# Fewer and later loads at the start of a fused encoder layer: constants packed into two arrays, one token block loaded after the first weights, 14 warming products instead of 17

## The chip, the cores and the metric

The kernel runs on one core of a Trainium2 chip. The metric is the device time of one execution in microseconds (us), lower is better. Before the change three runs gave a median of 1285.72 us (1284.95 to 1287.09).

## The reference

One encoder layer on x of 1024 tokens by 1024 features, all in float32:

```python
h = rmsnorm(x, norm1_w)
z = h @ w_in                     # 2852 columns, split into
qa, c_kv, iq, ik, iw, qb, kb, vb, gb = split(z)
c = rmsnorm(c_kv, kv_norm_w)
ka = rmsnorm(c @ w_uk, k_norm_w); va = c @ w_uv
out_a = indexed_sparse_attention(rmsnorm(qa, q_norm_w), ka, va, iq, ik, iw, rel_bias)
y = chunkwise_retention(rotary(qb), rotary(kb), vb)
out_b = silu(gb) * (group_norm(y) * ret_gn_w + ret_gn_b)
x = x + concat(out_a, out_b) @ w_out
h2 = rmsnorm(x, norm2_w)
return x + (silu(h2 @ w_gate) * (h2 @ w_up)) @ w_down
```

The sparse attention scores keys with a small indexer (`iq`, `ik`, `iw`), keeps 256 of them per query and attends over these.

## The kernel before, in words

The tokens are eight blocks of 128 (`NB`), worked in two halves of four. A product in float32 is split into three: an operand is written as a rounded part and a rest (`Thi` and `Tlo` for tokens, `whi` and `wlo` for weights), and TensorE (PE) takes `whi,Thi`, `wlo,Thi` and `whi,Tlo`. ScalarE (ACT) makes the rounded parts, VectorE (DVE) the rests. For one block and one chunk of weight columns this is 8 steps over the features of three products each, 24 in all (`token_major`, L467).

The input projection (`in_proj`, L1018) goes chunk by chunk over the columns of `w_in`: first the chunk `idx` of 292 columns (the latent for keys and values, and the indexer), then chunks of 256 columns. In each chunk the four blocks follow one another. The weights of a chunk come in pieces over SyncE's DMA queue (SP) into three buffers `wraw` (`pieces`, L278); the first chunk has four pieces of 292 KB, of which the last goes into a buffer named `sc`. A later chunk has two pieces of 512 KB.

Each token block has two loads: its transposed halves `xt` of 256 KB each (`x_load`, L410), which ACT scales by the norm's weights `n1` into `Thi` and DVE into `Tlo` (`scale_in`, L398), and its plain rows, two of 256 KB into the tiles `maA` (`x_stats`, L442), of which ACT takes the sums of squares and GpSimd (POOL) the reciprocal roots `rstd`. The projection's results for `idx` are scaled by `rstd` into a tile `ci` (`post_idx`, L477), and `keys` (L489) makes the keys of a block from it: a transpose by the identity `eye`, scaling by `kvw` into `ct`, a product with `wukv`, the tile `kv`, its sums of squares on ACT, a root on DVE and POOL (`rc`), the tile `kn` on DVE and two more transposes on PE.

Before the first weights arrive, `first_loads` (L172) gives PE 17 products of a tile of zeros (`WARM`, L30; the tile is `junk`). `second_loads` (L188) issues the other early loads on SP and `constants2` (L217) the tables for later stages on ACT's queue. `roots` (L211) multiplies `kw` and `kvw` by constants on DVE.

The order within an engine is set in two steps. The kernel's own planner estimates clocks and interleaves threads of work (`tick`, `step`) with the main products. The framework under it then orders the instructions of each engine. Loads take turns at eight semaphores: each issue waits until the load eight places before it has landed, whichever of the two queues that was on. Every engine and each queue works strictly in its order.

Of the kernel before, what the change touches and what calls it, by code (L numbers as in the profile page):

```python
# [16 lines left out]
NB = 8  # L17
KT = 8
# [8 lines left out]
NEG = -1.0e30  # L27
BIG = 3.0e38
SUB = 2
WARM = 17  # L30
VALUES, PAIRS, GATES = 4, 4, 2


# [10 lines left out]
def host_constants():  # L44
    f = np.float32
    pos = np.arange(S, dtype=np.float64)
    inv = 10000.0 ** (-np.arange(32, dtype=np.float64) / 32)
    ang = (pos.astype(f)[:, None] * inv.astype(f)[None, :]).astype(np.float64)
    cos = np.cos(ang).astype(f).reshape(NB, 128, 32).transpose(1, 0, 2)
    sin = np.sin(ang).astype(f).reshape(NB, 128, 32).transpose(1, 0, 2)  # L50
    lg = np.log1p(-(2.0 ** (-5.0 - np.arange(H, dtype=np.float64))))
    dq = np.exp((pos + 1.0)[:, None] * lg[None, :])
    dk = np.exp(-(pos + 1.0)[:, None] * lg[None, :]) * DH ** -0.5
    dec = np.concatenate([dq, dk], axis=1).astype(f).reshape(NB, 128, 16).transpose(1, 0, 2)
    bits = np.tile((np.uint32(1) << np.arange(32, dtype=np.uint32))[None, :], (128, 1))
    eye = np.eye(128, dtype=f)
    return {
        "cos": np.ascontiguousarray(cos), "sin": np.ascontiguousarray(sin),
        "dec": np.ascontiguousarray(dec), "bits": bits, "eye": eye,
        "causal": np.triu(np.ones((128, 128), f)),  # L60
    }

# [11 lines left out]
def layouts(host):  # L74


    x = host["x"].reshape(NB, 128, KT, 128)
    near = np.ascontiguousarray(host["rel_bias"][buckets()].transpose(0, 2, 1))
    return {"xt": np.ascontiguousarray(x.transpose(0, 3, 2, 1)).reshape(NB, 128, KT * 128),
            "n1": np.ascontiguousarray(host["norm1_w"].reshape(KT, 128).T),  # L80
            "n2": np.ascontiguousarray(host["norm2_w"].reshape(KT, 128).T), "near": near}

# [37 lines left out]
class Layer:  # L120
# [51 lines left out]
    def first_loads(self):  # L172
# [10 lines left out]
        p = self.pd()  # L183
        for _ in range(WARM):
            nc.tensor.matmul(p, warm[:, :128], warm[:, :512], start=True, stop=True)
        self.x_load(1, (nc.scalar, nc.scalar))

    def second_loads(self):  # L188
        nc, a = self.nc, self.a
        self.stats(0)  # L190
        self.x_load(2, (nc.sync, nc.sync))
        self.sqk = self.st([128, NB, 16], tag="sqk")
        nc.sync.dma_start(self.sqk, a["dec"])
# [1 line left out]
        self.x_load(3, (nc.sync, nc.sync))  # L195
        for b in (2, 3):
            self.go("root", self.x_stats(b))
        self.eye = self.sb([128, 128], tag="eye")
        nc.sync.dma_start(self.eye, a["eye"])
        self.kvw = self.sb([128, 1], tag="kvw")  # L200
        nc.sync.dma_start(self.kvw, a["kv_norm_w"].rearrange("o p -> p o"))
        self.wukv = self.sb([128, 128], tag="wukv")
        nc.sync.dma_start(self.wukv[:, :64], a["w_uk"][0])
        nc.sync.dma_start(self.wukv[:, 64:], a["w_uv"][0])
        self.kw = self.sb([128, 1], tag="kw")
        self.qw = self.sb([128, 1], tag="qw")
        for s in range(2):
            nc.sync.dma_start(self.kw[64 * s:64 * s + 64], a["k_norm_w"].rearrange("o p -> p o"))
            nc.sync.dma_start(self.qw[64 * s:64 * s + 64], a["q_norm_w"].rearrange("o p -> p o"))

    def roots(self):  # L211

# [3 lines left out]

    def constants2(self):  # L217
        nc, a = self.nc, self.a
        self.cos = self.st([128, NB, 32], tag="cos")
        self.sin = self.st([128, NB, 32], tag="sin")  # L220
        nc.scalar.dma_start(self.cos, a["cos"])
        nc.scalar.dma_start(self.sin, a["sin"])
        self.causal = self.st([128, 128], tag="causal")
        nc.scalar.dma_start(self.causal, a["causal"])
        self.gnw = self.st([128, 512], tag="gnw")
# [1223 lines left out]
```

## Time and profile before

| | |
|---|---|
| median of 3 runs | 1285.72 us |
| lowest, highest | 1284.95, 1287.09 us |
| the profiled execution | 1285.11 us |
| its span, first to last instruction | 1283.2 us |
| TensorE busy | 1252.7 us (98%) |
| VectorE, ScalarE busy | 992.2 us (77%), 785.9 us (61%) |
| mean granted TensorE clock | 0.999 |
| DMA, mean over the span | 95 GB/s, 121.34 MB |

The profile is of one execution. Its page gives busy times per engine; the trace behind it can be asked for instructions in order of time, with the idle time just before each and what ended it, and for the busy time of every engine in a chosen stretch. TensorE's busy time is modelled from pipelined products, so a product's printed length overlaps the next one; the distance from start to start is the better measure. The kernel's line for nearly all instructions is that of a helper (L100 before, L102 in the changed kernel), so groups are told apart by tile names.

### The profile page before, as it was taken

What the parts mean: (1) busy time and instruction counts of PE and PEld (TensorE: products, weight loads), DVE (VectorE), ACT (ScalarE), POOL (GpSimd) and SP (SyncE); (2) the same over time, 40 slices, a digit from 0 to 9 for tenths busy, and PEclk for the clock granted to TensorE, in tenths of its full rate; (3) what the DMA queues carried; (4) which work ended last, traced back from release to release, by engine and by line L of the source; (5) the groups of instructions that cost most, each with busy time, mean ns of one, the idle gap of its engine ahead of it and who ended that gap; (6) DMA issues with size and microseconds to landing.
All of it is one profiled execution on the core that took longest, in us unless ns stands there. A gap on an engine that the chain in (4) does not pass through costs nothing.

```text
span 1283.2 us, 22661 instructions
## 1 busy us (share of the span) xinstructions
PE 1252.7 (98%) x8369; PEld 1125.7 (88%) x8369; DVE 992.2 (77%) x2584; ACT 785.9 (61%) x1764; POOL 57.9 (5%) x68
## 2 busy tenths in 40 slices
PE   8999999999999999999999999999989999999998
PEld 6899998999999887888888878888988989898997
DVE  5889999888978887778887686545489787777883
ACT  7778986555795795588568834423385354444551
POOL 0501011010020000000000000000000000000000
PEclk9999999999999999999999999999999999999999
DMA  8523214221242223222222222225434242323302
GB/s 294 157 73 101 67 46 116 67 67 34 67 148 67 67 83 94 70 66 84 82 68 72 91 66 81 84 68 200 144 98 149 67 132 78 120 84 115 99 33 83
DMA packets 156895, 121.34 MB, mean 95 GB/s; under 512 B 7280, under 2 KB 136944, under 8 KB 156656
## 3 DMA queue, kind: packets, MB, share of 16 engines
q1 hardware_dynamic: 151744, 111.14, 28.9%
q10 hardware_dynamic: 5040, 8.74, 1.9%
q8 instruction: 66, 1.08, 0.4%
q14 instruction: 45, 0.37, 0.1%
HBM read 115.67 MB, written 4.19 MB: 93 GB/s over the span
## 4 chain that ended last, share of the span: by engine, by line
PE 59%; DVE 18%; ACT 14%; issue 5%; DMA 3%; POOL 1%; ACTq 0%; POOLq 0%; SPq 0%; DVEq 0%
PE d L100 50%; PE t L100 7%; ACT junk L100 6%; DVE wlo L100 4%; ACT whi L100 2%; PE l L100 2%; DVE L L100 2%; DMA wraw<-in_w_in_dram 1%; DVE S L100 1%; DVE Tlo L100 1%; ACT waste L100 1%; ACT Thi L100 1%; DVE th L100 1%; DVE wraw L100 1%; DVE junk L100 1%
## 5 line engine op out<-in xcount | busy, mean ns | idle before, releaser
L100 PE MATMUL d<-whi,Thi 128*128 128x256 f32 (+2 forms) x1136 | 349.5, 308 | 3.6 <-ACT whi L100 1.4
L100 PE MATMUL d<-wlo,Thi 128*128 128x256 f32 (+2 forms) x1136 | 340.0, 299 | 1.6 <-DVE wlo L100 1.6
L100 PE MATMUL d<-whi,Tlo 128*128 128x256 f32 (+2 forms) x1136 | 339.8, 299 | 0.0
L100 PEld LDWEIGHTS d<-whi,Thi 128*128 128x128 f32 x1136 | 214.2, 189 | 17.2 <-ACT Thi L100 2.2
L100 ACT ACTIVATE whi<-wraw 128x512 fp32r<-128x512 f32 (+1 forms) x300 | 172.8, 618 | 84.6 <-PE d L100 62.3
L100 PEld LDWEIGHTS d<-wlo,Thi 128*128 128x128 f32 x1136 | 214.5, 189 | 10.1 <-DVE wlo L100 2.3
L100 PEld LDWEIGHTS d<-whi,Tlo 128*128 128x128 f32 x1136 | 214.5, 189 | 8.7 <-DVE Tlo L100 1.2
L100 DVE TENSOR_TENSOR wlo<-wraw,whi 128x512 fp32r<-128x512 f32 (+1 forms) x302 | 197.2, 674 | 12.6 <-ACT whi L100 12.2
L100 ACT ACTIVATE junk<-sc,tc 128x384 bf16<-128x384 f32 (+5 forms) x186 | 163.5, 879 | 35.6 <-DVE tc L100 32.9
L100 PE MATMUL d<-Phi,wlo 128*128 128x256 f32 x616 | 170.8, 278 | 3.0 <-DVE wlo L100 3.0
L100 PE MATMUL d<-Phi,whi 128*128 128x256 f32 x616 | 171.3, 279 | 1.3 <-ACT u L100 1.0
L100 PE MATMUL d<-Plo,whi 128*128 128x256 f32 x616 | 170.7, 278 | 0.0
L100 PE MATMUL d<-Thi,whi 128*128 128x512 f32 (+1 forms) x368 | 143.0, 389 | 0.0
L100 PE MATMUL d<-Tlo,whi 128*128 128x512 f32 (+1 forms) x368 | 141.4, 385 | 1.3 <-DVE Tlo L100 1.3
L100 PE MATMUL d<-Thi,wlo 128*128 128x512 f32 (+1 forms) x368 | 141.4, 384 | 0.0
L100 PEld LDWEIGHTS d<-Phi,wlo 128*128 128x128 f32 x616 | 115.5, 188 | 3.7 <-DVE wlo L100 3.6
L100 PEld LDWEIGHTS d<-Phi,whi 128*128 128x128 f32 x616 | 115.9, 188 | 2.5 <-ACT u L100 1.7
L100 PEld LDWEIGHTS d<-Plo,whi 128*128 128x128 f32 x616 | 115.6, 188 | 0.3
L100 DVE TENSOR_TENSOR x<-d,x 128x512 f32<-128x512 f32 (+1 forms) x56 | 33.9, 614 | 64.5 <-PE d L100 56.7
L100 ACT ACTIVATE whi<-S 128x1024 fp32r<-128x1024 f32 x44 | 45.6, 1057 | 60.4 <-PE d L100 47.4
L100 PEld LDWEIGHTS d<-Thi,wlo 128*128 128x128 f32 x368 | 69.1, 188 | 14.8
L100 PEld LDWEIGHTS d<-Tlo,whi 128*128 128x128 f32 x368 | 69.2, 188 | 13.7 <-DVE Tlo L100 1.6
(331 smaller groups left out, 2349.0 us busy)
## 6 DMA issues: line engine op xcount, KB each, us to landing
wraw<-in_w_down_dram SPq DMA_DIRECT2D x44, 512.0 KB, 3.7
wraw<-in_w_in_dram SPq DMA_DIRECT2D x24, 512.0 KB, 3.7
wraw<-in_w_gate_dram SPq DMA_DIRECT2D x44, 256.0 KB, 3.1
wraw<-in_w_up_dram SPq DMA_DIRECT2D x44, 256.0 KB, 3.5
quad<-in_w_gate_dram SPq DMA_DIRECT2D x44, 256.0 KB, 3.6
quad<-in_w_up_dram SPq DMA_DIRECT2D x44, 256.0 KB, 4.0
wraw<-in_w_in_dram SPq DMA_DIRECT2D x32, 256.0 KB, 3.4
wraw<-in_w_out_dram SPq DMA_DIRECT2D x16, 512.0 KB, 4.2
```

The costliest lines, as they stand in the source:

```text
L100: return f(*args, **kw)
```

## The change

Eight loads of small constants (`eye`, `kvw`, the halves of `wukv`, and `kw` and `qw` twice each) become one array `few` of 128 by 259, put together on the host and loaded once. `cos` and `sin` become one array `turn`, and its load goes from ACT's queue to SP's. The two loads of token block 1 go from ACT's queue, before the weights' consumers, to SP's queue behind the four pieces of the first chunk. `WARM` goes from 17 to 14.

```diff
-WARM = 17
+WARM = 14
...
+    twice = lambda w: np.concatenate([w, w], axis=1).T
+    few = np.concatenate([np.eye(128, dtype=np.float32), host["w_uk"][0], host["w_uv"][0], host["kv_norm_w"].T,
+                          twice(host["k_norm_w"]), twice(host["q_norm_w"])], axis=1)
...
         for _ in range(WARM):
             nc.tensor.matmul(p, warm[:, :128], warm[:, :512], start=True, stop=True)
-        self.x_load(1, (nc.scalar, nc.scalar))
 
     def second_loads(self):
         nc, a = self.nc, self.a
+        self.x_load(1, (nc.sync, nc.sync))
         self.stats(0)
+        few = self.sb([128, 259], tag="few")
+        nc.sync.dma_start(few, a["few"])
+        self.eye, self.wukv = few[:, :128], few[:, 128:256]
+        self.kvw, self.kw, self.qw = [few[:, i:i + 1] for i in (256, 257, 258)]
         self.x_load(2, (nc.sync, nc.sync))
...
-        self.eye = self.sb([128, 128], tag="eye")
-        nc.sync.dma_start(self.eye, a["eye"])
-        self.kvw = self.sb([128, 1], tag="kvw")
-        nc.sync.dma_start(self.kvw, a["kv_norm_w"].rearrange("o p -> p o"))
-        self.wukv = self.sb([128, 128], tag="wukv")
-        nc.sync.dma_start(self.wukv[:, :64], a["w_uk"][0])
-        nc.sync.dma_start(self.wukv[:, 64:], a["w_uv"][0])
-        self.kw = self.sb([128, 1], tag="kw")
-        self.qw = self.sb([128, 1], tag="qw")
-        for s in range(2):
-            nc.sync.dma_start(self.kw[64 * s:64 * s + 64], a["k_norm_w"].rearrange("o p -> p o"))
-            nc.sync.dma_start(self.qw[64 * s:64 * s + 64], a["q_norm_w"].rearrange("o p -> p o"))
...
-        self.cos = self.st([128, NB, 32], tag="cos")
-        self.sin = self.st([128, NB, 32], tag="sin")
-        nc.scalar.dma_start(self.cos, a["cos"])
-        nc.scalar.dma_start(self.sin, a["sin"])
+        turn = self.st([128, 2, NB, 32], tag="turn")
+        nc.sync.dma_start(turn, a["turn"])
+        self.cos, self.sin = turn[:, 0], turn[:, 1]
```

The order of instructions moves on every engine up to the first chunks of the projection; TensorE's differs in some 430 rows at its head (of 7735 before and 7726 now) and is the same after them. Three places matter below.

First, SP's queue ahead of the second chunk of weights. Before, from the loads of token block 3 (`mb__171`, `mb__172`) to `qw`; the same two small loads `kw` and `qw` come once more and then the first piece of the second chunk, `wraw`:

```order
L100 DMA mb__171<-in_xt_dram 128x512
L100 DMA mb__172<-in_xt_dram 128x512
L100 DMA eye<-in_eye_dram 128x128
L100 DMA kvw<-in_kv_norm_w_dram 128x1
L100 DMA wukv<-in_w_uk_dram 128x64
L100 DMA wukv<-in_w_uv_dram 128x64
L100 DMA kw<-in_k_norm_w_dram 64x1
L100 DMA qw<-in_q_norm_w_dram 64x1
```

Now, from the first chunk's last piece (`sc`) on; `mb__154` and `mb__155` are token block 1, `mb__162` and on blocks 2 and 3:

```order
L102 DMA sc<-in_w_in_dram 128x2x292
L102 DMA mb__154<-in_xt_dram 128x512
L102 DMA mb__155<-in_xt_dram 128x512
L102 DMA maA<-in_x_dram 128x512 x2
L102 DMA few<-in_few_dram 128x259
L102 DMA mb__162<-in_xt_dram 128x512
L102 DMA mb__163<-in_xt_dram 128x512
L102 DMA sqk<-in_dec_dram 128x128
L102 DMA maA<-in_x_dram 128x512 x2
L102 DMA mb__170<-in_xt_dram 128x512
L102 DMA mb__171<-in_xt_dram 128x512
L102 DMA wraw<-in_w_in_dram 128x4x256 x2
```

Between `sc` and the second chunk's first piece there were 17 issues and are now 12; the chunk's two pieces, which had two loads of `maA` between them, now stand together.

Second, the start of ACT's order. Before:

```order
L100 DMA cos<-in_cos_dram 128x256
L100 DMA sin<-in_sin_dram 128x256
L100 ACT_TABLE_LOAD
L100 ACTIVATE ss_81<-half 128x1
L100 DMA mb__109<-in_xt_dram 128x512
L100 DMA mb__110<-in_xt_dram 128x512
```

Now:

```order
L102 DMA causal<-in_causal_dram 128x128
L102 DMA gnw<-in_ret_gn_w_dram 128x512
L102 ACT_TABLE_LOAD
L102 ACTIVATE ss_81<-half 128x1
L102 DMA gnb<-in_ret_gn_b_dram 128x512
L102 DMA n_468<-in_n_dram 128x8
```

The places of `cos`, `sin` and token block 1 are taken by `causal`, `gnw`, `gnb` and the second norm's weights `n_468`, which all stood behind the last token block's scaling before. By the turns at eight semaphores, the issue of `sc` on SP waited for `sin` before and waits for `gnw` now.

Third, TensorE at the last token block of the first chunk. Before, these products (292 columns) ran to their end, then those of the second chunk (256 columns) followed, and the transposes of block 0's keys `kn` stood 33 products into that chunk:

```order
L100 MATMUL d_548<-wlo_160,Thi_58 128x256
L100 MATMUL d_548<-whi_159,Tlo_59 128x256
L100 MATMUL t_400<-eye_175,kn_383 128x128 x2
L100 MATMUL t_438<-eye_175,ci_330 128x128
L100 MATMUL d_548<-whi_159,Thi_58 128x256
```

Now they stand three products into the last block of the first chunk (its bank is `d_381`), and products of the second chunk (bank `d_476`) are mixed into that block:

```order
L102 MATMUL d_381<-whi_126,Tlo_59 128x292
L102 MATMUL t_369<-few_160,kn_306 128x128 x2
L102 MATMUL t_418<-few_160,ci_307 128x128
L102 MATMUL d_476<-whi_152,Thi_58 128x256
L102 MATMUL d_381<-whi_126,Thi_58 128x292
L102 MATMUL d_381<-wlo_127,Thi_58 128x292
L102 MATMUL d_476<-wlo_153,Thi_58 128x256
L102 MATMUL d_476<-whi_152,Tlo_59 128x256
L102 MATMUL d_476<-whi_152,Thi_58 128x256
```

The key work of block 0 has moved ahead by a block and more; on ACT the squares of `ci` and of `kv` and the first piece of the second chunk stand ahead of the last token block's scaling, where they stood behind it.

## Rows read from the trace of the kernel before

**Rows 1.** The page's busy times: engine, busy us, share of the span, instructions.

```profile
PE 1252.7 (98%) x8369; PEld 1125.7 (88%) x8369; DVE 992.2 (77%) x2584; ACT 785.9 (61%) x1764; POOL 57.9 (5%) x68
```

**Rows 2.** Busy time by stretch, with granted clock, DMA share, GB/s.

```profile
core 0: us, PE busy (x) PEld busy (x) DVE busy (x) ACT busy (x) POOL busy (x), PEclk, DMA share, GB/s
8.30:11.50 3.20, 1.63 (x7) 0.89 (x6) 3.20 (x12) 2.28 (x7) 0.00 (x0) 1.00 1.06 396
11.50:20.00 8.50, 8.50 (x64) 8.32 (x64) 7.31 (x31) 8.49 (x29) 1.11 (x2) 1.00 0.69 208
15.00:19.00 4.00, 4.00 (x32) 3.83 (x30) 2.81 (x15) 3.99 (x14) 1.11 (x2) 1.00 0.33 63
20.00:32.00 12.00, 10.08 (x65) 9.38 (x64) 6.46 (x25) 9.25 (x29) 1.65 (x3) 0.86 1.06 362
28.00:30.00 2.00, 2.00 (x11) 2.00 (x11) 0.91 (x4) 1.52 (x5) 0.55 (x1) 0.56 1.11 375
32.00:48.00 16.00, 13.44 (x112) 12.73 (x111) 12.26 (x46) 11.52 (x39) 6.91 (x9) 1.00 0.70 219
100.00:150.00 50.00, 48.77 (x407) 46.01 (x407) 46.05 (x205) 43.51 (x137) 4.47 (x4) 1.00 0.30 85
```

**Rows 3.** Timeline, first 10 us: start us, us, engine, instruction, [idle before, what ended it].

```profile
1.17 0.46 ACTq L100 DMA_DIRECT2D sin<-in_sin_dram  x1
...
2.02 6.65 PE L100 MATMUL d<-junk 128*128 128x512 bf16 x17 [2.02 <-DVE tm L100]
...
5.08 0.37 SPq L100 DMA_DIRECT2D sc<-in_w_in_dram  x1
...
7.74 0.31 DVE L100 CAST whi<-wraw 128x292 fp32r<-128x292 f32 x1 [1.56 <-DMA wraw<-in_w_in_dram]
...
8.32 0.48 PE L100 MATMUL d<-whi,Thi 128*128 128x292 f32 x1
...
9.79 0.40 PE L100 MATMUL d<-wlo,Thi 128*128 128x292 f32 x1 [0.98 <-DVE wlo L100]
```

**Rows 4.** Timeline of SP's queue, 12 to 20 us.

```profile
12.63 0.33 SPq L100 DMA_DIRECT2D kvw<-in_kv_norm_w_dram  x1
...
17.37 0.51 SPq L100 DMA_DIRECT2D wraw<-in_w_in_dram  x1
...
18.99 0.38 SPq L100 DMA_DIRECT2D wraw<-in_w_in_dram  x1
```

**Rows 5.** Waits of SP's queue, first 60 us: total us, times, longest.

```profile
SPq L100 <- DMA sin<-in_sin_dram: 0.7, 1, 0.7
```

**Rows 6.** DMA issues, first 60 us: KB each, median us from issue to landing.

```profile
sc<-in_w_in_dram SPq DMA_DIRECT2D x1, 292.0 KB, 5.7
mb__109<-in_xt_dram ACTq DMA_DIRECT2D x1, 256.0 KB, 4.0
...
gnw<-in_ret_gn_w_dram ACTq DMA_DIRECT2D x1, 256.0 KB, 6.9
...
sin<-in_sin_dram ACTq DMA_DIRECT2D x1, 128.0 KB, 3.9
```

**Rows 7.** Timeline of TensorE, 25 to 34 us.

```profile
25.55 0.28 PE L100 MATMUL d<-whi,Tlo 128*128 128x256 f32 x1
27.20 0.38 PE L100 MATMUL d<-whi,Thi 128*128 128x256 f32 x1 [1.37 <-ACT whi L100]
...
32.12 0.28 PE L100 MATMUL d<-whi,Tlo 128*128 128x256 f32 x1
33.66 0.44 PE L100 MATMUL t<-eye,kn 128*128 128x128 f32 x2 [1.26 <-DVE rq L100]
```

**Rows 8.** Timelines of ScalarE and VectorE, 26 to 32 us.

```profile
26.52 0.63 ACT L100 ACTIVATE whi<-wraw 128x512 fp32r<-128x512 f32 x1 [1.93 <-DMA wraw<-in_w_in_dram]
...
31.84 0.17 DVE L100 TENSOR_SCALAR n<-n 128x8 f32<-128x8 f32 x1 [1.42 <-DMA n<-in_n_dram]
```

**Rows 9.** Timeline, 41 to 44 us: a later block's keys, ScalarE to TensorE.

```profile
41.83 0.21 ACT L100 ACTIVATION_READ_ACCUMULATOR waste<-kv 128x1 f32 x1
...
43.23 0.44 PE L100 MATMUL t<-eye,kn 128*128 128x128 f32 x2 [0.65 <-DVE kn L100]
```

More of the change, by code (lines that the diff above doesn't have):

```diff
@@ L55, in host_constants @@
     bits = np.tile((np.uint32(1) << np.arange(32, dtype=np.uint32))[None, :], (128, 1))
-    eye = np.eye(128, dtype=f)
     return {
-        "cos": np.ascontiguousarray(cos), "sin": np.ascontiguousarray(sin),
-        "dec": np.ascontiguousarray(dec), "bits": bits, "eye": eye,
+        "turn": np.ascontiguousarray(np.stack([cos, sin], axis=1)),
+        "dec": np.ascontiguousarray(dec), "bits": bits,
         "causal": np.triu(np.ones((128, 128), f)),
@@ L78, in layouts @@
     near = np.ascontiguousarray(host["rel_bias"][buckets()].transpose(0, 2, 1))
-    return {"xt": np.ascontiguousarray(x.transpose(0, 3, 2, 1)).reshape(NB, 128, KT * 128),
+    twice = lambda w: np.concatenate([w, w], axis=1).T
+    few = np.concatenate([np.eye(128, dtype=np.float32), host["w_uk"][0], host["w_uv"][0], host["kv_norm_w"].T,
+                          twice(host["k_norm_w"]), twice(host["q_norm_w"])], axis=1)
+    return {"few": np.ascontiguousarray(few), "xt": np.ascontiguousarray(x.transpose(0, 3, 2, 1)).reshape(NB, 128, KT * 128),
             "n1": np.ascontiguousarray(host["norm1_w"].reshape(KT, 128).T),
```

## The prediction

> **What bounds the kernel now.** The page comes first [rows 1]: TensorE is busy 98% of the span, so only time in which it stands still, or runs slowly, can be won. The stretches come second [rows 2], since the change moves nothing after the first chunks of the projection. Up to 48 us TensorE loses time in three places: 8.3 to 11.5 us (busy 1.63 of 3.2), 20 to 32 us (10.08 of 12, and the granted clock reads 0.86) and 32 to 48 us (13.44 of 16). Later it loses little (48.77 busy of 50 from 100 to 150 us). The reader is to look at TensorE's own timeline next [rows 7], and then at who was late [rows 8].
>
> The large loss is one piece of 8 us. The product at 25.55 is the 12th of the second chunk; the next starts at 27.20, because ACT got the chunk's second piece of weights only at 26.52 [rows 8]. The clock then falls: from 28 to 30 us it reads 0.56 on average, between its levels of 2.4 and 1.2 GHz, and only 11 products fit into 2 us [rows 2]. Then TensorE stands 1.26 us before the transposes of `kn` at 33.66 [rows 7]. That is not the price of the key work: DVE had stood 1.42 us on the landing of the second norm's weights (`n`), with the roots that `kn` needs queued behind them [rows 8]. From 25.55 to 33.66 are 8.11 us with 22 product starts in them. A product of this kind takes 0.12 us at full speed (112 in 13.44 us, 32 to 48 us [rows 2]), so 22 x 0.12 = 2.64 us were work and **5.47 us were lost**.
>
> Why the weights were late stands in SP's queue. Eight small loads stood from 12.04 to 17.37, each holding one of the eight turns; the DMA engines ran dry meanwhile (share 0.33 from 15 to 19 us [rows 2]). The pieces of the second chunk were issued at 17.37 and 18.99 only [rows 4], into the rush that followed.
>
> **The change part by part.** *Eight loads become one, `few`.* SP made 17 issues between `sc` at 5.08 [rows 3] and the chunk's first piece at 17.37 [rows 4], 0.72 us each. Now it makes 12: two for token block 1 and one for `few` added, eight removed. The first piece is then issued near 5.08 + 12 x 0.72 = 13.7 us and the second near 14.4, as they stand together. With the 7.5 us from issue to use that the second piece had before (18.99 to 26.52), it is there by 22 us. TensorE had used up all else by 25.83 [rows 7], and ACT needs the piece 0.7 us ahead of TensorE (26.52 to 27.20), at 25.1; so it is hidden with 3 us to spare, and if it came later than that, each us would return as a stand of TensorE.
>
> *The second norm's weights, `gnw`, `gnb` and `causal` at the head of ACT's queue.* They land long before anything uses them, so the 1.42 us of DVE go, and with them the 1.26 us of TensorE. With the piece in time and no stand there, nothing in this stretch remains to pull the clock down. I count the whole 5.47 us as won.
>
> *Block 1 behind the first chunk, 14 products of zeros.* Ahead of or beside the four pieces there stood 2448 KB (token block 0, the pieces, `cos`, `sin`, block 1) and now stand 2256 (`causal`, `gnw`, `gnb` for the last two): 192 KB less, at 396 GB/s [rows 2] 0.5 us. Against it, `sc` waits for `gnw` and no longer for `sin` [rows 5]. `sin` took 3.9 us from 1.17; `gnw` goes out in the same place with twice the bytes. The nearest row of its size at that time, `mb__109`, took 4.0 us [rows 6], so `sc` leaves 0.1 us later. I take 0.3 us as won, bounds 0 and 0.5. The Trainium skill (DMA: Bandwidth & Descriptors, Queues, rings and completion order) says that each DMA engine takes turns between the queues that have work for it; by that rule the weights come no earlier while ACT's queue is as full as before, and the sum would be 3.1 in place of 3.4; no row here shows the sharing. Block 1 itself is needed by ACT at about 11.2 us and lands 512 KB behind `sc`: 10.8 - 0.5 + 1.3 = 11.6 for its second half, which ACT reaches after 1.2 us of the first. Nothing waits.
>
> The 17 products of zeros take 6.65 us, 0.39 each [rows 3]; three fewer are 1.2 us less work. But the first real product waits for its weights, which DVE got at 7.74, and started at 8.32 [rows 3]. So they are worth 0, within a bound of 0.3 either way; what they may cost in clock is a rival.
>
> *`cos` and `sin` as `turn`* are on SP behind two pairs of `maA`, of which the second waits for ACT's squares of block 1 (about 20 us); the third chunk's weights are queued behind. TensorE wants them only after the second chunk's 96 products (11.5 us), near 38 us: 0.
>
> *What the new order adds.* The transposes of block 0's `kn` now stand three products into the last block of the first chunk. ACT has no slack there (8.49 busy of 8.5 [rows 2]), and the path from its sums of squares of `kv` to these transposes took 43.23 - 41.83 = 1.40 us [rows 9]. In the new order two squares of block 1, `ci`, `ct`, `kv` and half of block 2's scaling lie ahead of it. I expect TensorE to reach the transposes first and to stand for the path: 1.40 us. Behind them the last block's scaling now waits on ACT for the first weight piece, and the mixed products wait for rests from DVE. The nearest row is the first chunk's stand of the same kind, 0.98 us [rows 3]. New waits together: 1.40 + 0.98 = 2.4 us. Lower bound: the stand alone that a later `kn` cost, 0.65 [rows 9]. Upper bound: 1.40 and all that the first chunk lost, 3.2 - 1.63 = 1.57 [rows 2], and one more 0.65, that is 3.6.
>
> **The sum.** 5.47 + 0.3 - 2.4 = 3.4 us faster, between 5.47 + 0 - 3.6 = 1.9 and 5.47 + 0.5 - 0.65 = 5.3. The profiled execution took 1285.11 us, of which 1283.2 are the span; 1281.7 is to be compared with it. The median of the runs lies 0.6 higher, so **1282.3 us**.
>
> **The rivals.** *A, the clock falls elsewhere.* TensorE ends the zeros up to 1.2 us earlier and works thinly until 11.5; or it stands for 2.4 us near 20 to 24 us. For it: before, a thin stretch (25.83 to 28 us) did pull the clock down. Against it: 8.3 to 11.5 us did not, with half of it idle [rows 2]. The slow stretch cost is known: 0.14 of 12 us at half speed is 3.4 us of it; at 11 products in 2 us against 16.7, about 0.34 us per us, 1.2 us in all. That gives 3.4 - 1.2 = 2.2 us faster, 1283.5. The Trainium skill (TensorE: Matmul & The Clock Gate, the HAM clock gate) puts it the other way round, that "the default state is throttled, and activity releases the throttle"; that speaks against taking warming products away. The trace agrees as far as the fall after 26 us goes.
>
> *B, new waits take the place of the old.* The waits come to 3.6 and the clock falls in them, 1.2: 5.47 + 0.3 - 4.8 = 1.0 us faster, 1284.7. For it: ACT is full there. Against it: the products of the second chunk that are mixed in fill part.
>
> *C, slower: `gnw` holds up the weights.* All 128 rows of `gnw` come from one row of the array, and when loaded before it took 6.9 us against 4.0 for `mb__109` [rows 6], though in the rush after 20 us. Were it 6.9 us again from 1.17, `sc` would be issued at 8.07, 3.0 us later, with all of SP's queue behind it; TensorE's full run would begin at 14.5 in place of 11.5, with the clock lost as well. 5.47 - 2.4 - 3.0 - 1.2 = 1.1 us slower, 1286.8. It decides from a landing 2 us later than `sin`'s, and passes the bound of 0.2% only from 8.5 us after issue on.
>
> *D, the start is hidden anyway.* VectorE is busy 46.05 of 50 us from 100 to 150 [rows 2]; if the middle stages are set by its chain, a head start is given back there: 1285.7. Against it: TensorE is the fuller one (48.77), and VectorE's queue starts earlier too.
>
> **How the numbers follow.** Forecast 0.48, A 0.25, B 0.12, C 0.06, D 0.09. About 0.2% (2.6 us) is what a measurement of this kernel tells from no change. The forecast's own range, 1.9 to 5.3, lies over 2.6 for four fifths: 0.39. Of A two fifths, 0.10. Faster 0.49. Slower: of C a part and what I did not think of, 0.05. The same 0.46. Range: from the forecast's best, 1285.7 - 5.3 = 1280.4, with 0.2 for the spread of runs, 1280.2, up to D with half a us of spread, 1286.2; outside lie most of C and tails.
>
> **What would show it.** Right: SP issues the second chunk before 15 us and the DMA share stays near 1 up to there; TensorE has no idle of over 0.5 us between its 5th and 20th product of the second chunk and a granted clock of 1.00 from 8 to 48 us; no wait of DVE for `n`; the transposes of `kn` near 22 us, after an idle of 1 to 1.5 us; from 64 us on the same products 3 to 4 us earlier. Wrong: `gnw` landing after 6 us, `sc` issued after 6, a clock under 1.00 before 25 us, or idle of over 3.6 us in TensorE between 18 and 30 us.

## The result, and the profile after

The changed kernel is **slower**: 1293.26 us (median of 6 runs, 1292.09 to 1293.85) against 1285.62 us for the kernel before on the same chip (6 runs, 1282.8 to 1287.73). The ratio is 1.0062, with a 95% interval of 1.0051 to 1.0073: by it 8.0 us more (6.6 to 9.4) where 3.4 us less were forecast. The profiled execution took 1292.86 us.

The page of the kernel after, to be held against [rows 1]:

```profile
span 1290.7 us, 22644 instructions
PE 1262.0 (98%) x8366; PEld 1135.8 (88%) x8366; DVE 992.6 (77%) x2584; ACT 786.2 (61%) x1764; POOL 57.0 (4%) x68
```

TensorE is busy 9.3 us longer with three products fewer; VectorE and ScalarE are within 0.5 us of before. So most of the time was not lost to idling: products got slower, and the change alters no product but the three of zeros that it drops and the order of those at the start.

The start first. Stretches of the kernel after (the columns of [rows 2]: us, PE, PEld, DVE, ACT and POOL busy, granted clock, DMA share, GB/s):

```profile
8.30:11.50 3.20, 1.37 (x4) 0.88 (x4) 3.05 (x12) 3.09 (x10) 0.00 (x0) 0.67 1.07 381
11.50:20.00 8.50, 8.43 (x47) 8.11 (x48) 7.72 (x32) 7.08 (x24) 0.85 (x2) 0.72 1.00 342
20.00:32.00 12.00, 11.06 (x77) 9.73 (x76) 7.52 (x30) 9.90 (x31) 2.02 (x5) 1.00 0.80 247
32.00:48.00 16.00, 13.33 (x111) 12.72 (x110) 11.19 (x43) 14.06 (x45) 7.12 (x10) 1.00 0.70 209
```

From 20 to 32 us TensorE is busy 11.06 us at a clock of 1.00 where it was 10.08 at 0.86: the hole that the change was to close is closed. But from 11.5 to 20 us the clock now reads 0.72. The timelines of TensorE, of ScalarE and VectorE, and of SP's queue after tell how that began (compare [rows 3]):

```profile
2.02 5.13 PE L102 MATMUL d<-junk 128*128 128x512 bf16 x14 [2.02 <-DVE tm L102]
8.91 0.37 PE L102 MATMUL d<-whi,Thi 128*128 128x292 f32 x1 [1.76 <-ACT Thi L102]
10.50 0.61 PE L102 MATMUL d<-wlo,Thi 128*128 128x292 f32 x1 [1.22 <-DVE wlo L102]
...
12.64 0.45 PE L102 MATMUL d<-whi,Thi 128*128 128x292 f32 x1
12.89 0.45 PE L102 MATMUL d<-wlo,Thi 128*128 128x292 f32 x1
```

```profile
7.01 1.28 ACT L102 ACTIVATE Thi<-mb__83,n 128x128 fp32r<-128x128 f32 x4 [3.85 <-DMA n<-in_n_dram]
8.45 0.31 DVE L102 CAST whi<-wraw 128x292 fp32r<-128x292 f32 x1 [0.65 <-DMA wraw<-in_w_in_dram]
```

```profile
6.42 0.37 SPq L102 DMA_DIRECT2D sc<-in_w_in_dram  x1
...
14.76 1.09 SPq L102 DMA_DIRECT2D wraw<-in_w_in_dram  x2
```

And the waits of SP's queue and the landings after, first 60 us (the views of [rows 5, 6]):

```profile
SPq L102 <- DMA gnw<-in_ret_gn_w_dram: 2.3, 1, 2.3
```

```profile
gnw<-in_ret_gn_w_dram ACTq DMA_DIRECT2D x1, 256.0 KB, 5.2
n<-in_n_dram SPq DMA_DIRECT2D x1, 4.0 KB, 5.3
```

`gnw` took 5.2 us and landed near 1.17 + 5.2 = 6.4; SP waited 2.3 us for it (0.7 for `sin` before), and `sc` left at 6.42 where it had left at 5.08. The first norm's weights, 4 KB, took 5.3 us, and ACT stood 3.85 us for them (the same wait ended at 5.39 before). The first weights themselves came later too: VectorE began to round them (`whi`) at 8.45 where it had begun at 7.74. TensorE ended its zeros at 7.15 and stood 1.76 us. The row names `Thi`, but its first tile was ready before 7.5 us; what came last was `whi`, done at 8.76. After one product TensorE stood 1.22 us more. The clock fell between these two products: it reads 1.00 from 7.2 to 9.3 us, 0.53 from 9.3 to 10.5, 0.50 up to 16.2 and 1.00 after that. At 0.50, which is the level of 1.2 GHz, products at 12.64 and 12.89 are 0.25 us apart, where 0.134 is the distance at 2.4 GHz in the same stage. The second chunk's weights were issued at 14.76 and not at 17.37 and 18.99 [rows 4], as forecast.

The late start and the closed hole nearly cancel. The search for the selection's threshold on VectorE (a fixed landmark, before and after, by the view of its tile) begins at 78.4 us before and 79.5 us after and ends at 194.3 and 195.5: the changed start is 1.1 us behind in these two executions. The first product of the last stage starts 1.7 us later. Here are all products of that stage with the moving tile `Phi` and the stationary tile `whi` (kernel before, then after; by the view of the tile: count, min/median/max ns, first to last start in us):

```profile
L100 PE MATMUL d<-Phi,whi x616: 276/276/392, 935.9 to 1245.9; 128*128 128x256 f32 x154
```

```profile
L102 PE MATMUL d<-Phi,whi x616: 274/283/387, 937.6 to 1253.3; 128*128 128x256 f32 x154
```

The same 616 products take 310.0 us before and 315.7 us after, at a full clock and with no wait added. **1.7 us were lost up to 937 us, 5.7 us in this stage**, 7.4 together of the 7.5 by which the two spans differ. A stretch in which TensorE does nothing but this stage's products shows the rate (kernel before, then after):

```profile
1210.00:1230.00 20.00, 20.00 (x179) 20.00 (x178) 18.24 (x22) 12.85 (x18) 0.00 (x0) 1.00 0.18 53
```

```profile
1210.00:1230.00 20.00, 20.00 (x170) 20.00 (x169) 17.66 (x20) 12.46 (x17) 0.00 (x0) 1.00 0.26 78
```

170 products fit where 179 did: from start to start 119 ns in place of 113. The granted clock is 1.00 in both. Over the whole stage the distances of such products that follow one another without a stand average 114.8 ns before and 119.3 after, 8.0 us for the 1822 of them; about 2 us came back in shorter stands and in other products, which leaves the 5.7.

What differs is where the tiles lie. `eye`, `kvw`, `wukv`, `kw` and `qw` took 1120 bytes of each partition; `few` takes 1056 (259 float32, rounded up). Every tile allocated behind it begins 64 bytes lower. From the two programs' allocations (first byte in a partition, and that modulo 128):

```
        whi, wlo             Thi, Tlo            Phi            Plo
before  49984 68672 (64)     16512 32896 (0)     120064 (0)     148736 (0)
after   49984 68672 (64)     16512 32896 (0)     120000 (64)    148672 (64)
```

The second buffers of `whi` and `wlo` lie 9344 bytes further, at 64 modulo 128 as well. After the change the stationary and the moving tile of the last stage begin at the same place modulo 128 bytes; before, they were 64 bytes apart. Two theories follow. **Places**: the two tiles' places alone cost the 5.7 us. **The rest**: something else in the change (its order, the clock, another traffic) slows the last stage.

### The profile page after: what moved, and what is told of

It reads as the page before. It is cut to its first block, busy times and chain, and to the rows that moved or that the text cites. A ratio compares the mean times of both kernels' runs of the same rounds, so it can differ in the third digit from the quotient of the medians.

```text
span 1290.7 us, 22644 instructions
## 1 busy us (share of the span) xinstructions
PE 1262.0 (98%) x8366; PEld 1135.8 (88%) x8366; DVE 992.6 (77%) x2584; ACT 786.2 (61%) x1764; POOL 57.0 (4%) x68
## 4 chain that ended last, share of the span: by engine, by line
PE 62%; DVE 17%; ACT 13%; issue 4%; DMA 2%; POOL 1%; SPq 0%; ACTq 0%; POOLq 0%; DVEq 0%
PE d L102 53%; PE t L102 7%; ACT junk L102 6%; DVE wlo L102 3%; DVE L L102 2%; PE l L102 2%; ACT whi L102 2%; DVE Tlo L102 1%; ACT waste L102 1%; DVE zqk L102 1%; DVE junk L102 1%; DVE wraw L102 1%; DVE S L102 1%; DVE tr L102 1%; ACT Thi L102 1%
## 5 line engine op out<-in xcount | busy, mean ns | idle before, releaser
L102 PE MATMUL d<-Phi,wlo 128*128 128x256 f32 x616 | 173.7, 283 | 2.2 <-DVE wlo L102 2.2
L102 PE MATMUL d<-Phi,whi 128*128 128x256 f32 x616 | 174.2, 283 | 1.0 <-ACT u L102 1.0
L102 PE MATMUL d<-Plo,whi 128*128 128x256 f32 x616 | 173.6, 282 | 0.0
```

The source lines that it names most:

```text
L102: return f(*args, **kw)
```

## Experiments: where the tiles lie

Medians over all runs of each kernel and of the kernel before on the same chip. `Phi` and `whi` are the first bytes of these tiles modulo 128 (0 and 64 before). The stage's length is the distance from first to last start in the view of its tile (310.0 before):

```
run                          us       before   ratio  interval        Phi  whi  stage us
change                       1293.26  1285.62  1.0062 1.0051..1.0073   64   64   315.7
e1_few280                    1286.35  1284.82  1.0012 1.0002..1.0022    0   64   309.2
e2_before_phi192             1289.77  1284.82  1.0042 1.0027..1.0057   64   64   315.3
e3_before_phi128             1284.07  1284.82  0.9994 0.9985..1.0003    0   64   308.8
e4_few_whi128                1294.3   1284.82  1.0077 1.0062..1.0092    0    0   316.4
e8_whi128_phi64              1287.96  1284.99  1.0027 1.0016..1.0039   64    0   311.1
e12_before_phi32             1290.13  1284.94  1.0036 1.0022..1.0049   32   64   315.2
```

**The changed kernel with the old places.**

```diff
-        few = self.sb([128, 259], tag="few")
-        nc.sync.dma_start(few, a["few"])
+        few = self.sb([128, 280], tag="few")
+        nc.sync.dma_start(few[:, :259], a["few"])
```

> The changed kernel with the tile of the constants 84 bytes a partition wider, so that every tile behind it lies where it lay before the change; nothing else moves. Address theory: of the 7.6 us lost, 5.4 come from the last stage's products, whose moving operands Phi and Plo lay 64 bytes lower; they start again mostly 0.113 us apart and not 0.120, and the kernel takes about 1287.8 us (2.2 slower than before). Rival (the last stage was slow because of something that the new start brings, a clock or a phase): 1293 us again, products 0.120 apart.

The stage went back to 309.2 us and the time to 1.0012 of before. Every engine's order is that of the changed kernel; nothing but the places changed, so *the rest* falls. What is left, 1.5 us, is the start.

**The kernel before with the new places**, and as a control with a shift by a whole 128 bytes (`[128, 32]`):

```diff
+            self.st([128, 48], tag="pad")
             self.Phi = self.st([128, 7, 4, 256], F32R, tag="Phi")
```

> The kernel before with 192 unused bytes ahead of Phi in the last stage, so that Phi and Plo start 192 bytes past a multiple of 256, as in the changed kernel; the start is as before. Address theory: products of the last stage 0.120 us apart, 5.4 us slower than before, about 1291. Rival (the new start is the cause): 1285.6, as before.

> The kernel before with 128 unused bytes ahead of Phi: 128 past a multiple of 256. If a multiple of 128 is what counts: as before, 1285.6, products mostly 0.113 apart. If it must be 256: slower by up to 5.4 us, 1291. Rival (addresses do not matter): 1285.6 and the same spacing in all three kernels of this call that move Phi.

192 unused bytes, and not one instruction changed, cost 5.3 us in the stage (315.3 against 310.0) and 1.0042 in all. 128 bytes cost nothing. So a shift by 128 doesn't matter, and one by 64 (modulo 128) does.

**Is it a matter of `Phi`'s place, or of both tiles'?** The next run moves `whi` and `wlo` up by 64 and keeps `Phi` at its good place (with the first experiment's start).

```diff
         self.rq = self.sb([128, NB, 8], tag="rq8")
+        self.sb([128, 16], tag="pad")
```

> The changed kernel with 64 unused bytes ahead of the weight tiles whi and wlo, which then start at multiples of 128 and not 64 past one; Phi and Plo lie as before the change. Address theory: the last stage recovers its 5.4 us, and products whose moving operand is whi or wlo (the projections) come from 0.117 nearer to 0.113 apart, up to 4 us more: 1284 to 1287.8. Rival (start or phase is the cause): 1293.

This expectation failed: with every tile at a multiple of 128 the stage was slow again (316.4), and so were, a little, the 256-column products of the projection (stationary `Thi`, at 0 too): from 100 to 170 us the mean length of `wlo,Thi` rose from 283 ns to 285, and behind 60 us the median from start to start from 117 to 120. (Up to 1.7 us of the 316.4 go to a stretch at half clock: it reads 0.75 from 952 to 956 us and 0.82 from 956 to 960. The next run's profile has such a stretch too, and its 311.1 are to be read so.) So a good start in itself isn't what counts; the two tiles' places against each other must. That was tested by moving `Phi` by 64 as well:

```diff
+            self.st([128, 16], tag="pad5")
             self.Phi = self.st([128, 7, 4, 256], F32R, tag="Phi")
```

> The kernel of the fourth experiment (changed kernel, all from whi on 64 bytes higher: whi and wlo begin at a multiple of 128 bytes) with 64 unused bytes ahead of Phi, so that Phi and Plo begin 64 bytes off a multiple of 128. Theory (a product is slow where its stationary and its moving tile begin at the same place modulo 128 bytes, fast where they differ by 64): the products of Phi and Plo are 113 to 114 ns apart again although both tiles changed their places, those of Thi stay at 120, and the last stage gives back 5.4 to 6 us of the fourth experiment's 1294.3: 1288.5 us. Rival (Phi and Plo themselves must begin at a multiple of 128): 120 ns and 1294 us.

The stage's rows of the fourth experiment and of this one:

```profile
L102 PE MATMUL d<-Phi,whi x616: 274/283/415, 938.5 to 1254.9; 128*128 128x256 f32 x154
```

```profile
L102 PE MATMUL d<-Phi,whi x616: 276/276/415, 940.2 to 1251.3; 128*128 128x256 f32 x154
```

Modulo 128 `Phi` now stands where it had been slow in the changed kernel, and is fast, because `whi` moved as well: the theory's 113 ns came (179 products from 1210 to 1230 us, 170 in the fourth experiment), and the time fell to 1287.96. A last run asked how near the two places may be:

```diff
+            self.st([128, 8], tag="pad")
             self.Phi = self.st([128, 7, 4, 256], F32R, tag="Phi")
```

> The kernel before with 32 unused bytes ahead of Phi: Phi and Plo begin 32 bytes past a multiple of 128, whi and wlo 64 past one as ever. If only tiles that begin at the same place modulo 128 bytes are slow together, the products of Phi and Plo stay at 113 to 114 ns and the time at 1285 us. If it is the half of 128 bytes that counts, the same (Phi lies in the other half than whi). If each byte nearer to whi costs its share, they are at 116 to 118 ns and the time is 2 to 3 us longer, 1287.5 us. If a tile off a multiple of 64 bytes is slow in itself, they are at 120 ns or more and 1290 us or more.

```profile
L100 PE MATMUL d<-Phi,whi x616: 276/281/388, 934.0 to 1249.2; 128*128 128x256 f32 x154
```

32 bytes apart is as slow as 0 (315.2 us). The median lies at 281 ns and the rate at 170 in 20 us, so the expectation's two middle cases both missed; whether 32 is slow by its distance from `whi` or because it is no multiple of 64 isn't told apart. Of the distances tried in this stage, 64 modulo 128 is fast, 0 and 32 are slow. The size doesn't carry over as it is: in the projection `whi` (at 64) and `Thi` (at 0) are 64 apart in the kernel before, yet these products are 117 to 118 ns apart at the median, not 113, and 120 with both at 0. Why the same distance gives less there no run tells.

## Experiments: the start

With the places put right the change still loses 1.5 us (e1) where 3.4 were to be won. The theories: **late weights** (`gnw` and `gnb`, 512 KB on ACT's queue, hold up the first weights and `sc`), **zeros** (three fewer let the clock fall), and **hidden** (a lead at the start doesn't reach the end). All kernels here have the padded `few`.

```
run                               us       before   ratio  interval
e5_few280_gn_late                 1286.76  1284.99  1.0014 1.0005..1.0022
e6_few280_17zeros                 1287.08  1284.99  1.0014 1.0005..1.0023
e7_few280_gn_late_17zeros         1284.68  1284.99  1.0002 0.9993..1.0011
e9_gn_behind_bits                 1285.47  1284.94  0.9999 0.9990..1.0008
e10_gn_behind_bits_3_more_zeros   1285.13  1284.94  1.0000 0.9992..1.0009
e11_gn_behind_bits_17zeros        1286.15  1284.94  1.0008 0.9999..1.0017
e13_before_with_few               1283.42  1284.48  0.9992 0.9983..1.0001
e14_before_with_few_n2_first      1284.1   1284.48  0.9997 0.9988..1.0006
```

The edits of e5 to e7 (e5: the loads alone; e6: `WARM = 17` alone; e7: both):

```diff
-        nc.scalar.dma_start(self.gnw, a["ret_gn_w"].to_broadcast([128, 512]))
-        nc.scalar.dma_start(self.gnb, a["ret_gn_b"].to_broadcast([128, 512]))
+        nc.sync.dma_start(self.gnw, a["ret_gn_w"].to_broadcast([128, 512]))
+        nc.sync.dma_start(self.gnb, a["ret_gn_b"].to_broadcast([128, 512]))
...
-        nc.scalar.dma_start(bias, a["near"])
+        nc.sync.dma_start(bias, a["near"])
```

> The kernel of the first experiment (changed kernel, few padded so that later addresses are those of before), with gnw and gnb issued on SP behind turn and the bias table on SP too, so that ACT's queue begins with four small loads (causal, n2, bits, far). Theory (the late start is gnw's and gnb's 512 KB ahead of the weights): sc leaves near 5.1 us instead of 6.3, the first norm's weights land near 5.3 instead of 6.9, the first real product starts near 8.0 to 8.3 instead of 8.57; 1285.0 us, 1.3 less than the first experiment's 1286.35. If the low clock from 12.3 to 15.7 us came from the late start as well, it goes too, and the time is 1283.3. Rival (the three missing products of zeros cost the clock): the clock still reads about 0.7 to 0.8 from 11.5 to 20 us and only the 1.3 come back. Second rival (the start is hidden later): 1286.3, as the first experiment.

> The kernel of the first experiment with 17 products of zeros again. If the three missing products cost the clock, the window 11.5 to 20 us reads 1.00 (0.8 to 0.85 in the first experiment), the products there are 0.134 us apart throughout, and about 15 x 0.11 = 1.7 us come back: 1284.7 us. If the late weights cost the clock, the fall from 12.3 to 15.7 us stays and the time is 1286.3. If 17 products end after the first weights are there, the first real product starts later by up to 0.2 us.

> Both: gnw, gnb and bias off the head of ACT's queue, and 17 products of zeros. Theory of two separate costs (late weights 1.3 us, clock 1.7 us): sc near 5.1 us, first product near 8.3 us, clock 1.00 from 8 to 48 us, 1286.35 - 3.0 = 1283.3 us, that is about 1.5 below the kernel before on the same chip, and the kernel is 1 to 3 us ahead of before at 69 us. Rival (the start is hidden by the middle stages): no more than 0.5 below the first experiment.

*Late weights* holds at the start itself. Without the 512 KB on ACT's queue (e5) the first product starts 1.2 us sooner than in the first experiment (8.57), and the second hardly waits for its rest:

```profile
2.02 5.67 PE L102 MATMUL d<-junk 128*128 128x512 bf16 x14 [2.02 <-DVE tm L102]
7.34 0.48 PE L102 MATMUL d<-whi,Thi 128*128 128x292 f32 x1
8.02 0.40 PE L102 MATMUL d<-wlo,Thi 128*128 128x292 f32 x1 [0.20 <-DVE wlo L102]
```

With 14 zeros its clock reads 1.00 up to 48 us, so three zeros fewer don't bring the low clock by themselves. But the time didn't fall: 1286.76, where 1285.0 or less was expected. In e6 three more zeros did keep the clock at 1.00 from 11.5 to 20 us (0.80 in e1), as one of its theories had it, and the 1.7 us that this was to give back didn't come either: 1287.08. In e7, of which 1283.3 was expected, the profile tells where the lead went. From 20 to 48 us its TensorE is busy 25.59 of 28 us at a clock of 1.00, against 23.52 at 0.94 before. Counting the real products, each at its distance in the kernel before, it is about 3.4 us ahead at 48 us (the forecast's size), 2 us ahead at 140, and 1.4 behind at 260. The search (kernel before, then e7: first step, last step):

```profile
L100 DVE TENSOR_TENSOR tc<-tm,bits x1: 143/143/143, 78.4 to 78.4; 128x2 uint32<-128x2 uint32 x1
L100 DVE TENSOR_SCALAR tv<-tc x1: 160/160/160, 194.3 to 194.3; 128x2 f32<-128x2 f32 x1
```

```profile
L102 DVE TENSOR_TENSOR tc<-tm,bits x1: 155/155/155, 75.9 to 75.9; 128x2 uint32<-128x2 uint32 x1
L102 DVE TENSOR_SCALAR tv<-tc x1: 159/159/159, 196.9 to 196.9; 128x2 f32<-128x2 f32 x1
```

It begins 2.5 us sooner and ends 2.6 us later: 121.0 us in place of 115.9. These edits change what the planner counts, and with it the order up to some 220 us; in this order ACT and VectorE do other work between the steps. From 180 to 210 us VectorE is busy 28.79 of 30 us (28.10 before), so nothing there can be caught up. In e5, whose `gnw`, `gnb` and `bias` are moved in the same way, the search takes 121.2 us too. That the longer search is the cause of the loss fits in place and size, but no run took it away; about 1 us of the 3.4 lost between 140 and 260 us goes with a stretch at half clock near 208 us (the clock reads 0.91 from 200 to 220), and e2 and e3, with the same reading, lose as much there. In the sixth experiment, whose order is another, the search takes 116.1 us, and the time is no better: its lead of about 3 us at 44 us was gone by 60 us.

So the next runs leave the order alone. `gnw` and `gnb` go behind `n2` and `bits` on their own queue (TensorE's order is then the first experiment's, product for product); e10 adds three zeros that the planner doesn't count, e11 counts them.

```diff
-        nc.scalar.dma_start(self.gnw, a["ret_gn_w"].to_broadcast([128, 512]))
-        nc.scalar.dma_start(self.gnb, a["ret_gn_b"].to_broadcast([128, 512]))
...
         nc.scalar.dma_start(self.bits, a["bits"])
+        nc.scalar.dma_start(self.gnw, a["ret_gn_w"].to_broadcast([128, 512]))
+        nc.scalar.dma_start(self.gnb, a["ret_gn_b"].to_broadcast([128, 512]))
```

> The kernel of the first experiment with gnw and gnb only moved behind n2 and bits on ACT's own queue; TensorE's order is the first experiment's, product for product. Theory (gnw ahead of the first norm's weights and sc costs the start; an order kept as it was lets the gain reach the end): gnw is issued near 3.9 us instead of 1.17, sc leaves near 5.1 us instead of 6.3, the first norm's weights land near 5.3, the first real product starts near 8.0, the selection's search starts near 78.6 and takes 116 us as in the kernel before, and the end comes 1.3 us sooner than in the first experiment, at 1285.0 us; 1283.4 if the low clock from 12.3 to 15.7 us goes as well. Rival (the 512 KB are as much in the way from 3.9 us as from 1.2): sc after 6 us and 1286.3 us.

> The same with three more products of zeros that the planner isn't charged for, so that TensorE's order behind them stays the first experiment's. Theory: the clock reads 1.00 from 8 to 20 us, TensorE is 2 us or more ahead of the kernel before at 48 us, the search starts 2 us sooner than in the kernel before (near 76.5) and takes 116 us, and a lead of about 2 us reaches the end: 1283.0 us. Rival (any lead is lost between 160 and 240 us, where VectorE is busy 9 to 10 us of 10, whatever the order): a lead at 140 us and none at 300 us, 1285 us.

> gnw and gnb behind bits on ACT's queue, and 17 products of zeros that the planner counts: its order is the one that the sixth experiment had, not the seventh's. Theory (the order decides what becomes of the lead): sc near 5.1 us, first product near 8 us, the search takes 116 us as in the sixth experiment and not the 121 us of the seventh, and the time is 1283 to 1284 us. Rival: the lead is lost near 55 us as in the sixth experiment, 1286 us.

`sc` left at 5.06 and ACT had the first norm's weights at 4.83, as expected, and yet the first product of e9 started at 8.72, waiting for the first weights:

```profile
8.72 0.37 PE L102 MATMUL d<-whi,Thi 128*128 128x292 f32 x1 [1.89 <-DVE whi L102]
```

`gnw` was now issued at 2.15 us and not at 3.9, beside the weights. So it isn't only the shared semaphore: the first weights come late also where `sc` leaves early. The start of VectorE's first rounding of weights (`whi`), in all executions with a profile, shows what goes with it (us; in e5 and e14 VectorE came to it without a stand, so there the weights may have landed earlier):

```
ACT's queue at the start                        VectorE has the first weights at
four small loads (e5, e7)                       5.97 6.30
cos, sin, block 1 (before, e2, e3, e12 to e14)  7.74 7.37 6.64 7.33 7.52 6.88
n2, bits, then gnw, gnb (e9 to e11)             8.26 7.94 7.62
gnw, gnb, then n2 (after, e1, e4, e6, e8)       8.45 8.11 8.62 7.74 8.28
```

The means are 6.1, 7.2, 7.9 and 8.2: with `gnw` and `gnb` at the head the first weights come 1.0 us later than in the kernel before. The 0.3 us between the last two rows lie within the spread of single executions. Whether it is their bytes or that all their rows are read from one row of the array wasn't tried. In time e9 and e10 equal the kernel before; against e1 e9 is 0.0013 less, about as much as the two intervals together leave open. Three more zeros did nothing to the time (1285.13 and 1285.47). None of the leads came that these three runs were to show: e10 is level with the kernel before from 44 us on, and e11, 2 us ahead at 48 us, has lost it by 100; its 1286.15 is its rival's 1286 and not the 1283 to 1284 of its theory.

**The low clock near 12 us.** All sixteen executions with a profile can be sorted by what TensorE did between the zeros and the first product (us that it stood; the granted clock from 11.5 to 20 us, in the same order):

```
zeros  TensorE stood before the first product             clock
14     1.76 1.66 2.35 1.27 1.89 (after, e1, e4, e8, e9)   0.72 0.80 0.80 0.69 0.80
14     not at all (e5)                                    1.00
17     0.59 0.38 (e2, e12)                                0.80 0.80
17     not at all (before, e3, e6, e7, e10, e11, e14)     1.00 in each
17     not at all (e13)                                   0.82
```

Where it stood, the clock was low in seven of seven; where the zeros lasted to the first product, in one of nine. Three more zeros closed the stand in e6 (against e1) and in e10 (against e9), and the clock stayed up. It is one execution of each, and the time didn't follow: the half-clock stretch came later, near 55 us in e6 and 24 us in e10.

**The largest term by itself**: the kernel before with the eight loads replaced by `few`, nothing else. e14 also issues `n2` ahead of `causal`, `gnw` and `gnb`.

> The kernel before with the eight small loads replaced by few (padded, so that all later addresses stay), at few's place in the changed kernel; cos, sin, token block 1, 17 products of zeros and gnw as before. It tests the largest term of the sum by itself: 5.47 us lost between 25.55 and 33.66 us in the kernel before, of which the late second chunk is the cause. If the term holds, the second chunk's first piece is issued near 14 us, TensorE has no stand of over 0.5 us at its 12th product, and the time is 2 to 4 us less than the kernel before: 1282 us. If the low clock only moves to another place of the start and the wait for the second norm's weights stays, 1 us less: 1284 us. If the order that the planner makes of it loses the lead by 300 us, as in the seventh experiment, 1285 us.

> The same, with the 4 KB of the second norm's weights issued ahead of causal, gnw and gnb instead of behind them. If DVE's wait for them (1.42 us near 31 us in the kernel before) stands in TensorE's way, the transposes of kn come 1.3 us sooner and the time is 1 us less than in the experiment with few alone; if not, the same time as there.

1.0 us less, by its interval between 2.2 less and 0.1 more. The pieces were issued at 12.28 and 15.62, the timeline shows no stand of TensorE between 11.06 and 29.89 us, and it was about 1.9 us ahead at 140 us. The low clock had moved: 0.82 from 11.5 to 20 us. That is the time of the expectation's middle case, but only half of its reason: VectorE's wait for the second norm's weights was gone. So e14, which issues `n2` first, had nothing left to win, and made no difference. e13 is the fastest version that the parts gave; it is not told apart from the kernel before, let alone by 0.2%.

**What one profile of the start is worth.** The kernels of e2, e3 and e12 have the instructions of the kernel before, one for one, up to the last stage. Their profiles don't agree about the start. The kernel before, e12 and e3, same three stretches (the clock is the third number from the end):

```profile
12.00:16.00 4.00, 4.00 (x32) 4.00 (x31) 3.92 (x14) 4.00 (x14) 0.26 (x1) 1.00 0.95 323
28.00:32.00 4.00, 3.79 (x18) 3.50 (x19) 1.33 (x8) 3.24 (x11) 1.10 (x2) 0.57 1.07 380
32.00:36.00 4.00, 2.74 (x23) 2.44 (x22) 2.87 (x15) 1.87 (x7) 1.27 (x2) 1.00 0.58 193
```

```profile
12.00:16.00 4.00, 4.00 (x21) 4.00 (x20) 3.62 (x14) 3.99 (x15) 0.55 (x1) 0.57 0.93 321
28.00:32.00 4.00, 1.99 (x15) 1.58 (x14) 2.11 (x12) 2.53 (x9) 1.53 (x4) 1.00 1.04 354
32.00:36.00 4.00, 4.00 (x35) 3.88 (x34) 3.47 (x12) 3.76 (x13) 0.60 (x2) 1.00 0.46 140
```

```profile
12.00:16.00 4.00, 4.00 (x32) 4.00 (x31) 3.25 (x13) 3.99 (x14) 0.55 (x1) 1.00 0.89 309
28.00:32.00 4.00, 1.67 (x12) 1.33 (x11) 2.01 (x12) 2.42 (x9) 1.39 (x3) 0.97 1.08 378
32.00:36.00 4.00, 4.00 (x23) 4.00 (x23) 3.12 (x9) 3.21 (x10) 0.43 (x1) 0.61 0.38 122
```

Each of these three has one stretch at half clock in the first 48 us, and each at another place (e2 has two, at 12 and at 32 us); in e12 it falls at 12 us with 17 zeros ahead of it. The search begins at 78.4, 76.5 and 77.2 us (77.7 in e2). The profile on which the forecast was built was the latest of the four, by 1.9 us from the first. All leads given above are against it: e12 has one of 1.9 us at 140 us with nothing changed at the start, so a lead of that size in a single profile, e13's too, shows no gain.

## Why the prediction was wrong, point by point

**The step that failed** is the sentence "the change moves nothing after the first chunks of the projection", and with it a sum that ended at 48 us. The order of the instructions after the start is the same, but `few` moved every tile behind it by 64 bytes, and that cost 5.7 us in the last stage (5.3 when done alone, in e2). No rival held it either: all four were about the start. Shown by e1, e2, e4 and e8. It is not the whole miss: of the 11.4 us between forecast and result the places are 6.4, and with them put right the change still loses 1.5 us (e1) where 3.4 were to be won. Those 4.9 us are terms of the sum, below. The prediction's own signs of being wrong told of the start: `gnw` landed after 6 us, `sc` was issued after 6, the clock was under 1.00 before 25. None of its signs looked past the start's first products but one (the same products 3 to 4 us earlier from 64 us on), and none at the last stage.

- **"I count the whole 5.47 us as won"**: mis-sized. The cause was read right: with `few` the second chunk comes in time, and the hole from 25.55 to 33.66 us is gone. Alone in the kernel before it measures 1.0 us (0.1 more to 2.2 less). Of the 5.47 us about 1.7 were a half-clock stretch (0.57 over the 4 us from 28) that other executions of the same instructions have elsewhere, so it only moved. In the changed kernel, by the count of products, TensorE is 2.7 us behind at 24 us, even at 36 and 1.0 behind at 48: there 2.7 us were won back, and went to make up for the start.
- **"I take 0.3 us as won, bounds 0 and 0.5"** for block 1 behind the first chunk: wrong in sign. The first product came 0.6 us later (8.91 against 8.32) and the first full run of products ran at half clock. This is rival C's mechanism: `gnw` took 5.2 us and not the 4.0 of `mb__109`, and `sc` left 1.3 us later. That C's 1.1 us slower lie near e1's 1.5 is luck: C had `sc` 3.0 us later and all of the 5.47 won. It was given 0.06; the row that spoke for it, 6.9 us in [rows 6], had been set aside as taken in a rush. The bytes were counted before `sc` in all, but not those that ran beside the first piece.
- **The queues' turns.** These runs show what no earlier row did: VectorE has the first weights at 6.1 us on average with small loads alone on ACT's queue, and at 7.2 to 8.2 with large ones. The rule of the Trainium skill (DMA: Bandwidth & Descriptors, Queues, rings and completion order) is that each DMA engine takes turns between the queues that have work for it. The runs agree with it, though none tells turns from another kind of sharing. By it the forecast would have been 0.3 less (3.1 in place of 3.4). The price measured, `gnw` and `gnb` in place of what stood there, is 1.0 us.
- **The zeros, "worth 0, within a bound of 0.3"**: holds for the time (e9 and e10 are alike). Rival A's mechanism came true at the start of the changed kernel: the zeros ended 1.5 us earlier, the weights came later, TensorE stood between them, and the clock fell. The three zeros were part of it (e9 against e10, e1 against e6), but not alone: with 14 zeros and early weights it stays (e5), with 17 it falls in e2, e12 and e13. What else it turns on isn't settled. A's price, 1.2 us for a low clock moved elsewhere, can't be read off: the low stretch is in the kernel before as well.
- **"New waits together: 1.40 + 0.98 = 2.4 us"**: the transposes of `kn` stood 0.65 us at 25.30, not 1.40 near 22, and no second stand of 0.98 followed. Over-sized by 1.7 us.
- **Rival D**, the start is hidden anyway: not settled. Leads of about 3.4 us (e7, at 48 us) and 3 (e6, at 44) were gone by 260 us. But e12, whose order is that of the kernel before, keeps its 1.9 us from 36 us to the last stage, so a lead isn't lost wherever VectorE is busy. That the new order of e5 to e7 decides it is argued, not shown.

By the medians the change comes to: `few` 1.0 us less, the rest of the start +2.6 (e1 less e13), the places +6.4 (the change less e1; 5.7 in the profiles), each from the ratios: 8.0 in all. By the intervals each of the three is good to between 1 and 2 us.

## What to carry to other kernels

A smaller tile moves all tiles behind it. When a change touches an allocation, compare the first bytes of the tiles that the longest stage reads, before any sum is made over the instructions that moved; and when the time can't be explained, pad the tile to its old size and run again. What a change can win back of a loss read from the start of one profile may be far less (1.0 of 5.47 us here): look at a second execution for what of it stays in place.

## What the runs showed of the hardware that was not expected

In the last stage TensorE's 256-column float32 products, each with another stationary tile, run 179 in 20 us where the stationary and the moving tile begin 64 bytes apart modulo 128 and 170 where they begin 0 or 32 apart, at the same granted clock of 1.00: 113 against 119 ns from start to start. In the projection the median is 117 to 118 ns where the two tiles begin 64 apart and 120 where they begin 0 apart. Products of 512 columns don't show it: those of `whi` and `hh` have a median of 393 ns before and 394 in the fourth experiment. The Trainium skill (TensorE: Matmul & The Clock Gate, Step-by-step: what each phase is for) says that the two operands come through independent read ports, so that loading the next stationary tile takes nothing from the running product. Here the measurement differs: the rate depends on how the two tiles lie to each other, by 6 ns in 113. Whether that is in the two reads, or where else, no run here shows.
